# One pool of eight PSUM banks, and the transposes of a head pair in one run, in a two-layer hybrid attention block

## The chip, the cores and the metric

The kernel runs on one core of a Trainium2 chip. The metric is the device time of one execution in microseconds (us), the median of three runs. Engines are named as in the profile: PE (TensorE matmuls), PEld (TensorE weight loads), DVE (VectorE), ACT (ScalarE), POOL (GpSimd), SP (SyncE, whose queue issues the DMAs).

## The reference

The block has two layers over 256 tokens `x` and 256 context tokens `ctx`, 1024 features, float32. Each layer normalises and modulates its input, projects it, and computes three branches: neighbourhood attention with a bias (NA, 8 heads of 64), a gated MLP with spatial mixing, and latent attention (MLA, 8 heads of 96). The branches are merged by sigmoid gates, and a squared-ReLU MLP follows. The last layer updates only `x`. What the change touches is the softmax attention of both kinds:

```python
def dense_attention(q, k, v):
    ...
        s = jnp.einsum('bhqd,bhkd->bhqk', q_blk, k).astype(jnp.float32) * scale
        p = jax.nn.softmax(s, axis=-1).astype(v.dtype)
        return jnp.einsum('bhqk,bhkd->bhqd', p, v)
```

In layer 0 the 256 `x` queries see 512 keys (context and `x`) and the 256 context queries see the 256 context keys; in layer 1 there are only the `x` queries.

## The kernel before

**Tiles and stages.** Tokens are handled in tiles of 128. Every projection is three float32r matmuls per 128 rows of contraction (`mm3`, L286 to L289: high by high, high by low, low by high), with the weights split into a rounded part on ACT (L115) and a rest on DVE (L116). A layer runs: key, query and value projections (`gemm_b`, L305), the MLA latents, the gated MLP (`u` L716, `sg` L724), NA attention (L740 to L753), part of the merge (L757), the MLA keys and queries (L760 to L837), MLA attention (L842 to L849), the rest of the merge (L852 to L856), the output projection with the next norm (L887 to L914), and the MLP (L943 to L972).

**Attention.** `soft_pv` (L427) handles one pair of heads. For each stream `v` (stream 0: `x` queries with 4 key tiles; stream 1, in layer 0 alone: context queries with 2) and each query tile `qt` it writes the scores of both heads to PSUM (tile `S`, L438: two float32r matmuls per head in NA, L410 and L411; one float32 matmul per head, shown as two records, in MLA, L417). Then for each head: bias add on DVE (L443, NA and stream 0 alone), negated row maximum on DVE (L445), exponential with its sum on ACT (L448), reciprocal and scaling on DVE (L450, L451), transposes of the 2 or 4 key tiles on PE into a bank `pt` (L454), and a copy to the tile `PT` on ACT (L456). I call the two heads of one `qt` of one stream a unit. After both units of a stream the values are applied (L460, `pv` or `pvm`, 16 records for four key tiles and 8 for two), behind the copy of the last head (the dependency at L464). `P` and `PT` have two buffers each.

**Banks.** PSUM has eight banks of 128x512. `psum(tag, name)` (L47) takes one from a pool with four tags:

```python
return pp.tile([128, 512], F32, tag=tag, name=name, bufs={"mm": 4, "s": 2, "pt": 1, "pv": 1}[tag])
```

Tag `mm` serves all projections (`b_ps`, `u`, `gate`, `z`, `kv`, `qm`, `o_ps`, `f`) and the modulation sums; `s` serves the scores, the norm's sums `st_ps`, and all small transposes (`mod_t`, `tr_ps`, `c_tr`, `h_tr`) and `sg`; `pt` the transposed probabilities; `pv` the attention output and the broadcast norm `rstd_b`.

**What sets the order of the work.** A scheduler in the tile framework, run when the program is built, orders the instructions of each engine: of those that are ready, the one that the program traced first. Each engine then works its list in that order. Tiles of one tag get their banks in the order in which the program first writes them: the first write of a tile is not put ahead of the first write of an earlier tile of the same tag, even if banks are free. Tiles of other tags may pass. Matmuls that add to a tile which has been written already are not bound by this.

**What stands beside attention.** `merge` (L474) computes for each of eight output tiles a gate (24 matmuls, L488) and a `z` (12 matmuls, L492), all in tag `mm`. The merges are traced after the four head pairs, and each of their steps is queued behind the scores of a certain unit (`paced`, L301, with `tc.issue_after` in `gemm_a`, L298; the first 10 or 36 steps are free), so that they spread over the attention.

**The norm.** `norm_apply` (L279) and `norm_stream` (L232) reduce the sums of squares with a matmul (`st_ps`, L237), form the factor (DVE L239, POOL L241, DVE L244), and broadcast it with a matmul (`rstd_b`, L247). In the output projection (L887 to L914) and at the end of layer 0's MLP (L965 to L972) the norm of stream 0 is traced between the chunks of stream 0 and those of stream 1, and that of stream 1 after them. `mod_pooled` (L177) forms layer 1's modulation beside layer 0's MLP; its two ends put matmuls, two copies (L214) and transposes (L217) into PSUM tiles.

Of the kernel before, what the change touches and what calls it, by code (L numbers as in the profile page):

```python
# [7 lines left out]
F32 = mybir.dt.float32  # L8
F32R = mybir.dt.float32r
AF = mybir.ActivationFunctionType  # L10
ALU = mybir.AluOpType
# [15 lines left out]
def hybrid_block_kernel(tc, a, out):  # L27
    nc = tc.nc
    act = nc.scalar.activation
    vec = nc.vector  # L30
    mm = nc.tensor.matmul

    from contextlib import ExitStack, nullcontext
    with ExitStack() as es:
        def pool(name, bufs=1, **kw):
            return es.enter_context(tc.tile_pool(name=name, bufs=bufs, **kw))
# [8 lines left out]
        pp = pool("ps", space=PSUM)  # L45

        def psum(tag, name):  # L47
            return pp.tile([128, 512], F32, tag=tag, name=name, bufs={"mm": 4, "s": 2, "pt": 1, "pv": 1}[tag])


        def g2(name, dt=F32R):
# [21 lines left out]
        ident = cp.tile([128, 128], F32, name="ident")  # L73
# [66 lines left out]
        def mod_finish(ps, w, dsts, modT, bmod, streams):  # L140

            t = tmp2("mod_sb")
            vec.tensor_copy(t[:, :w], ps[:, :w])
            pst = psum("s", "mod_t")
            for i in range(w // 128):
                nc.tensor.transpose(pst[:, i * 128:(i + 1) * 128], t[:, i * 128:(i + 1) * 128], ident)
            for i in range(w // 128):
                v4 = pst[:, i * 128:(i + 1) * 128].rearrange("p (j r) -> p j r", j=4)
                for v in range(streams):
                    o, b = dsts(modT[:, v, :], i), dsts(bmod, i)  # L150
                    i0 = v4[:, :, v]
                    if len(o.shape) == 3:
                        i0 = i0.rearrange("p (a b) -> p a b", a=2)
                    vec.tensor_tensor(out=o, in0=i0, in1=b, op=ALU.add)

        def mod_quarter(l, q, modT, bmod, streams):

            ps = psum("pt", "mod_ps")
            for kb in range(4):
                for kk in range(2):  # L160
                    raw = g2("rawm", F32)
                    nc.sync.dma_start(out=raw, in_=a["wmod1"][l, q, kb][:, kk * 512:kk * 512 + 512])
                    mod_cols(ps, raw, 0, 128, 2 * kb + kk)
                yield
            mod_finish(ps, 128, lambda m, i: m[:, 0:16].rearrange("p (a c) -> p a c", a=2)[:, :, 2 * q:2 * q + 2], modT,
                       bmod, streams)

        def mod_group(l, g, modT, bmod, streams):
            ps = psum("mm", "mod_ps")
            for k in range(KC):  # L170
                raw = load(a["wmod"][l, g - 2, k])
                mod_cols(ps, raw, 0, 256, k)
                yield
            mod_finish(ps, 256, lambda m, i: m[:, 8 * g:8 * g + 8].rearrange("p (j i) -> p j i", i=2)[:, :, i], modT, bmod,
                       streams)
# [251 lines left out]
        def soft_pv(score, V, pv, streams, bias, marks):  # L427

            for v in range(streams):
                kts = [0, 1, 2, 3] if v == 0 else [2, 3]  # L430
                k0, nk = kts[0] * 128, 128 * len(kts)
                PT = [gp.tile([128, 4, NX], F32, tag="PT", name="PT", bufs=2) for _ in range(2)]
                for qt in range(2):
                    q0 = v * NX + qt * 128
                    S = []
                    for hh in range(2):
                        s = psum("s", "S")
                        marks.append(score[hh](s[:, :nk], q0, k0, nk).ins)  # L438
                        S.append(s)
                    for hh in range(2):  # L440
                        s = S[hh]
                        if bias is not None and v == 0:
                            vec.tensor_tensor(out=s[:, :NX], in0=s[:, :NX], in1=bias[hh][:, qt, :], op=ALU.add)  # L443
                        nm = sp.tile([128, 1], F32, tag="nm", name="nm")
                        vec.tensor_reduce(out=nm, in_=s[:, :nk], axis=AX.X, op=ALU.max, negate=True)  # L445
                        P = gp.tile([128, 512], F32, tag="P", name="P", bufs=2)
                        sm = sp.tile([128, 1], F32, tag="sm", name="sm")
                        act(out=P[:, :nk], in_=s[:, :nk], func=AF.Exp, bias=nm, accum_out=sm)  # L448
                        r = sp.tile([128, 1], F32, tag="r", name="r")
                        vec.reciprocal(r, sm)  # L450
                        vec.tensor_scalar(out=P[:, :nk], in0=P[:, :nk], scalar1=r, scalar2=None, op0=ALU.mult)  # L451
                        pt = psum("pt", "pt")
                        for i in range(len(kts)):
                            nc.tensor.transpose(pt[:, i * 128:(i + 1) * 128], P[:, i * 128:(i + 1) * 128], ident)  # L454
                        n = len(kts)
                        turned = act(out=PT[hh][:, :n, qt * 128:(qt + 1) * 128],  # L456
                                     in_=pt[:, :nk].rearrange("p (i q) -> p i q", i=n), func=AF.Copy)
                for i, kt in enumerate(kts):
                    for hh in range(2):
                        m = mm(pv[64 * hh:64 * hh + 64, v * NX:(v + 1) * NX], lhsT=V[kt][hh], rhs=PT[hh][:, i, :],  # L460
                               start=(i == 0), stop=(i == len(kts) - 1), tile_position=(0, 64 * hh))
                        if i == 0 and hh == 0:

                            tc.add_manual_dep(m.ins, turned.ins.name, mybir.DependencyInfo(  # L464
                                mybir.DependencyClass.Sync, mybir.DependencyReason.DATA), reason="both heads")
# [81 lines left out]
        for l in range(L):  # L547
# [114 lines left out]
            for t in range(4):  # L662
                vec.tensor_scalar(out=cnat[t][:, 0:128], in0=cnat[t][:, 0:128], scalar1=rsc[:, t:t + 1], scalar2=None,
                                  op0=ALU.mult)
                if t in tts:
                    vec.tensor_scalar(out=cnat[t][:, 160:416], in0=cnat[t][:, 160:416], scalar1=rsc[:, 4 + t:5 + t],
                                      scalar2=None, op0=ALU.mult)
# [72 lines left out]
            for j in range(4):  # L740
                bias = []
                for hh in range(2):
                    bt = gp.tile([128, 2, NX], F32, tag="bias", name="bias", bufs=2)
                    with tc.issue_after(last_load[0]):
                        nc.sync.dma_start(out=bt, in_=a["nab"][l, 2 * j + hh])
                    bias.append(bt)
                pv = psum("pv", "pv")
                soft_pv([na_score(kT, qT, 2 * j + hh) for hh in range(2)],
                        [[vna[t][:, (2 * j + hh) * 64:(2 * j + hh + 1) * 64] for hh in range(2)] for t in range(4)],
                        pv, ns, bias, marks)  # L750
                H, Lo = split_out(pv, "yna", T)
                ynH.append(H)
                ynL.append(Lo)  # L753
# [88 lines left out]
            for j in range(4):  # L842
                pv = psum("pv", "pvm")
                soft_pv([mla_score(kmT, qmT, 2 * j + hh) for hh in range(2)],
                        [[vml[t][:, (2 * j + hh) * 64:(2 * j + hh + 1) * 64] for hh in range(2)] for t in range(4)],
                        pv, ns, None, marks)
                H, Lo = split_out(pv, "yml", T)
                ymH.append(H)
                ymL.append(Lo)  # L849
# [36 lines left out]
            both = BOTH if ns == 2 else 0  # L886
# [11 lines left out]
            for n in range(both, 8):  # L898
                out_chunk(a["wa"][l, 28 + n], n, mixH, mixL, [0], 16, acc)
                if last:  # L900
# [3 lines left out]
                                             op0=ALU.mult, op1=ALU.subtract)  # L904
# [165 lines left out]
```

## Time and profile before

| | us |
|---|---|
| median of 3 runs (lowest to highest) | 1402.77 (1400.9 to 1403.62) |
| the profiled execution's own time | 1402.83 |
| its span in the trace | 1400.8 |
| PE busy | 1370.2 (98%) |
| DVE busy | 957.4 (68%) |
| ACT busy | 704.7 (50%) |

The span is the time from the first to the last instruction; 2.0 us of the profiled execution lie around it. PE's busy time counts a matmul to its modelled end, and a matmul overlaps the next one's start, so the start-to-start distances of a timeline are the finer measure. A line of the timeline reads: start, duration, engine, line of the kernel, operation, written and read tiles, shape, count, and in brackets idle time with what ended it.

### The profile page before, as it was taken

What the parts mean: (1) busy time and instruction counts of PE and PEld (TensorE: products, weight loads), DVE (VectorE), ACT (ScalarE), POOL (GpSimd) and SP (SyncE); (2) the same over time, 40 slices, a digit from 0 to 9 for tenths busy, and PEclk for the clock granted to TensorE, in tenths of its full rate; (3) what the DMA queues carried; (4) which work ended last, traced back from release to release, by engine and by line L of the source; (5) the groups of instructions that cost most, each with busy time, mean ns of one, the idle gap of its engine ahead of it and who ended that gap; (6) DMA issues with size and microseconds to landing.
All of it is one profiled execution on the core that took longest, in us unless ns stands there. A gap on an engine that the chain in (4) does not pass through costs nothing.

```text
span 1400.8 us, 22572 instructions
## 1 busy us (share of the span) xinstructions
PE 1370.2 (98%) x8438; PEld 1161.8 (83%) x8438; DVE 957.4 (68%) x2071; ACT 704.7 (50%) x1440; POOL 56.9 (4%) x35
## 2 busy tenths in 40 slices
PE   6999999999999999999999999999999999999999
PEld 4788767777676789988888888988888878999998
DVE  4666477665563558899766665786787766877775
ACT  3466256443453346623324233566676665656654
POOL 0110000110000000000000000011002100000000
PEclk9999999999999999999999999999999999999999
DMA  9423542234313465665555552443543434566664
GB/s 331 142 84 106 187 150 90 71 105 123 119 46 114 127 195 168 208 202 172 203 205 188 175 197 89 150 137 94 181 136 99 136 91 136 181 181 180 183 183 148
DMA packets 67214, 210.61 MB, mean 150 GB/s; under 512 B 8609, under 2 KB 9633, under 8 KB 67105
## 3 DMA queue, kind: packets, MB, share of 16 engines
q1 hardware_dynamic: 67104, 209.18, 46.6%
q8 instruction: 66, 1.08, 0.3%
q14 instruction: 44, 0.35, 0.1%
HBM read 208.10 MB, written 1.05 MB: 149 GB/s over the span
## 4 chain that ended last, share of the span: by engine, by line
PE 96%; DVE 1%; DMA 1%; ACT 1%; issue 0%; SPq 0%; POOL 0%; ACTq 0%; DVEq 0%
PE o_ps L287 8%; PE o_ps L289 8%; PE o_ps L288 8%; PE f L288 6%; PE f L287 6%; PE f L289 6%; PE gate L287 5%; PE gate L288 5%; PE gate L289 5%; PE b_ps L287 5%; PE b_ps L288 4%; PE b_ps L289 4%; PE pt L454 3%; PE S L417 2%; PE z L287 2%; PE z L289 2%
## 5 line engine op out<-in xcount | busy, mean ns | idle before, releaser
L115 ACT ACTIVATE wh<-raw 128x512 fp32r<-128x512 f32 (+1 forms) x570 | 353.1, 626 | 515.8 <-PE o_ps L288 179.7
L116 DVE TENSOR_TENSOR wl<-raw,wh 128x512 fp32r<-128x512 f32 (+1 forms) x570 | 385.8, 683 | 178.1 <-ACT wh L115 172.7
L289 PE MATMUL f<-hH,wl 128*128 128x258 f32 (+2 forms) x560 | 180.9, 324 | 0.1
L287 PE MATMUL f<-hH,wh 128*128 128x258 f32 (+2 forms) x560 | 180.4, 323 | 0.5 <-ACT wh L115 0.5
L288 PE MATMUL f<-hL,wh 128*128 128x258 f32 (+2 forms) x560 | 180.4, 324 | 0.2 <-DVE hL L277 0.2
L288 PE MATMUL o_ps<-aL,wh 128*128 128x256 f32 (+1 forms) x544 | 176.1, 327 | 0.0
L287 PE MATMUL o_ps<-aH,wh 128*128 128x256 f32 (+1 forms) x544 | 176.0, 328 | 0.0
L289 PE MATMUL o_ps<-aH,wl 128*128 128x256 f32 (+1 forms) x544 | 175.6, 328 | 0.0
L287 PE MATMUL gate<-hH,wh 128*128 128x512 f32 (+1 forms) x384 | 140.5, 366 | 0.0
L289 PE MATMUL gate<-hH,wl 128*128 128x512 f32 (+1 forms) x384 | 130.3, 339 | 0.0
L288 PE MATMUL gate<-hL,wh 128*128 128x512 f32 (+1 forms) x384 | 130.1, 339 | 0.0
L287 PEld LDWEIGHTS f<-hH,wh 128*128 128x128 f32 x560 | 106.0, 190 | 9.1 <-ACT wh L115 0.7
L289 PEld LDWEIGHTS f<-hH,wl 128*128 128x128 f32 x560 | 106.2, 190 | 8.5 <-DVE wl L116 0.3
L288 PEld LDWEIGHTS f<-hL,wh 128*128 128x128 f32 x560 | 105.9, 190 | 8.5 <-DVE hL L277 0.4
L287 PEld LDWEIGHTS o_ps<-aH,wh 128*128 128x128 f32 x544 | 102.7, 190 | 9.5 <-ACT aH L937 0.8
L288 PEld LDWEIGHTS o_ps<-aL,wh 128*128 128x128 f32 x544 | 103.1, 190 | 8.5
L289 PEld LDWEIGHTS o_ps<-aH,wl 128*128 128x128 f32 x544 | 102.7, 190 | 8.8
L288 PE MATMUL b_ps<-wl,hH 128*128 128x512 f32 (+2 forms) x288 | 108.8, 381 | 0.0
L289 PE MATMUL b_ps<-wh,hL 128*128 128x512 f32 (+2 forms) x288 | 106.3, 381 | 0.0
L287 PE MATMUL b_ps<-wh,hH 128*128 128x512 f32 (+2 forms) x288 | 103.7, 385 | 0.0
L200 DVE SCALAR_TENSOR_TENSOR macc<-rawx,sS,macc 128x512 f32<-128x512 f32 x112 | 78.9, 748 | 32.7 <-DMA rawx<-in_wmod_dram 32.4
L287 PEld LDWEIGHTS gate<-hH,wh 128*128 128x128 f32 x384 | 72.7, 189 | 15.9 <-issue 7.5
(229 smaller groups left out, 2481.3 us busy)
## 6 DMA issues: line engine op xcount, KB each, us to landing
raw<-in_wa_dram SPq DMA_DIRECT2D x147, 512.0 KB, 3.6
raw<-in_w_dram SPq DMA_DIRECT2D x68, 512.0 KB, 3.6
raw<-in_wb_dram SPq DMA_DIRECT2D x32, 512.0 KB, 3.3
raw<-in_wmod_dram SPq DMA_DIRECT2D x32, 512.0 KB, 3.4
rawx<-in_wmod_dram SPq DMA_DIRECT2D x32, 512.0 KB, 4.5
raw<-in_wo_dram SPq DMA_DIRECT2D x24, 512.0 KB, 3.6
rawm<-in_wmod_dram SPq DMA_DIRECT2D x32, 256.0 KB, 6.0
rawx<-in_wmod_dram SPq DMA_DIRECT2D x32, 256.0 KB, 4.2
```

The costliest lines, as they stand in the source:

```text
L115: act(out=wh[:, :width], in_=src, func=AF.Copy)
L116: vec.tensor_tensor(out=wl[:, :width], in0=src, in1=wh[:, :width], op=ALU.subtract)
L200: summed = vec.scalar_tensor_tensor(out=o, in0=src, scalar=s, in1=o, op0=ALU.mult, op1=ALU.add)
L287: mm(ps, lhsT=sh, rhs=mh, start=first, stop=False)
L288: mm(ps, lhsT=sh, rhs=ml, start=False, stop=False)
L289: mm(ps, lhsT=sl, rhs=mh, start=False, stop=last)
L417: return mm(s, lhsT=Q[h][0:96, q0:q0 + 128], rhs=K[h][0:96, k0:k0 + nk], start=True, stop=True)
L454: nc.tensor.transpose(pt[:, i * 128:(i + 1) * 128], P[:, i * 128:(i + 1) * 128], ident)
```

## The change

All PSUM tiles come from one tag with eight banks. In `soft_pv` the loop over the two heads is cut in two: the first does bias, maximum, exponential and scaling of both heads; the second does the transposes and copies of both. The first transpose of the unit gets a dependency on the scaling of the second head.

```diff
-            return pp.tile([128, 512], F32, tag=tag, name=name, bufs={"mm": 4, "s": 2, "pt": 1, "pv": 1}[tag])
+            return pp.tile([128, 512], F32, tag="bank", name=name, bufs=8)
...
+                    Ps = []
                     for hh in range(2):
                         s = S[hh]
...
-                        vec.tensor_scalar(out=P[:, :nk], in0=P[:, :nk], scalar1=r, scalar2=None, op0=ALU.mult)
+                        scaled = vec.tensor_scalar(out=P[:, :nk], in0=P[:, :nk], scalar1=r, scalar2=None, op0=ALU.mult)
+                        Ps.append(P)
+                    for hh in range(2):
+                        P = Ps[hh]
                         pt = psum("pt", "pt")
                         for i in range(len(kts)):
-                            nc.tensor.transpose(pt[:, i * 128:(i + 1) * 128], P[:, i * 128:(i + 1) * 128], ident)
+                            m = nc.tensor.transpose(pt[:, i * 128:(i + 1) * 128], P[:, i * 128:(i + 1) * 128], ident)
+                            if i == hh == 0:
+
+                                tc.add_manual_dep(m.ins, scaled.ins.name, mybir.DependencyInfo(
+                                    mybir.DependencyClass.Sync, mybir.DependencyReason.DATA), reason="both heads")
```

## Rows read from the trace of the kernel before

**Rows 1.** The page: busy time by engine, and the clock in 40 slices.

```profile
PE 1370.2 (98%) x8438; PEld 1161.8 (83%) x8438; DVE 957.4 (68%) x2071; ACT 704.7 (50%) x1440; POOL 56.9 (4%) x35
...
PEclk9999999999999999999999999999999999999999
```

**Rows 2.** Windows, four attention stretches; columns: width, busy PE, PEld, DVE, ACT, POOL, PEclk.

```profile
185.00:262.00 77.00, 73.95 (x438) 52.40 (x437) 58.09 (x155) 50.39 (x130) 3.63 (x2) 1.00 0.29 96
340.00:446.00 106.00, 106.00 (x573) 74.53 (x572) 55.52 (x136) 49.48 (x122) 0.00 (x0) 1.00 0.29 93
1015.00:1068.00 53.00, 49.11 (x350) 41.11 (x351) 39.75 (x98) 36.86 (x85) 1.85 (x2) 1.00 0.37 108
1105.00:1165.00 60.00, 56.34 (x379) 42.87 (x378) 34.84 (x77) 35.84 (x82) 0.00 (x0) 1.00 0.26 79
```

**Rows 3.** Layer 0: the last query parts on DVE, then PE's timeline before attention.

```profile
L401 DVE SCALAR_TENSOR_TENSOR naQL<-tr_ps,gq,naQ x16: 743/750/757, 100.3 to 119.1; 64x512 fp32r<-64x512 f32 x16
...
173.24 1.05 PE L724 MATMUL sg<-wsT,gv 128*128 128x128 f32 x8
...
174.79 0.51 PE L287 MATMUL gate<-hH,wh 128*128 128x512 f32 x1
...
181.54 0.39 PE L410 MATMUL S<-naK,naQ 128*128 128x512 f32 x1
```

**Rows 4.** One tile's instructions (`pt`): transposes and copies; ns min/median/max.

```profile
L454 PE MATMUL pt<-ident,P x320: 269/273/333, 189.7 to 1159.9; 128*128 128x128 f32 x160
L456 ACT ACTIVATE PT<-pt x96: 364/597/602, 190.3 to 1160.2; 128x512 f32<-128x512 f32 x64, 128x256 f32<-128x256 f32 x32
```

**Rows 5.** Timeline: one NA head with four key tiles, layer 1's last pair.

```profile
1055.30 0.48 PE L410 MATMUL S<-naK,naQ 128*128 128x512 f32 x1
...
1056.05 0.43 DVE L443 TENSOR_TENSOR S<-S,bias 128x256 f32<-128x256 f32 x1 [0.20 <-PE S L411]
...
1056.52 0.69 DVE L445 TENSOR_REDUCE nm<-S 128x1 f32<-128x512 f32 x1
...
1059.26 0.68 ACT L448 ACTIVATE P<-S,nm 128x512 f32<-128x512 f32 x1
...
1060.97 0.63 PE L454 MATMUL pt<-ident,P 128*128 128x128 f32 x4 [0.89 <-DVE P L451]
...
1062.28 1.95 PE L460 MATMUL pv<-PT,vna 128*64 128x256 f32 x16 [0.69 <-ACT PT L456]
```

**Rows 6.** Timeline: one MLA head's scores and their maximum, layer 1.

```profile
1154.38 1.02 PE L417 MATMUL S<-kml,qml 96*128 96x512 f32 x2
...
1155.44 0.69 DVE L445 TENSOR_REDUCE nm<-S 128x1 f32<-128x512 f32 x1 [0.60 <-PE S L417]
```

**Rows 7.** Timeline: NA heads with two key tiles, layer 0.

```profile
216.28 0.28 PE L411 MATMUL S<-naK,naQL 128*128 128x256 f32 x1
...
216.60 0.42 DVE L445 TENSOR_REDUCE nm<-S 128x1 f32<-128x256 f32 x1 [1.13 <-PE S L411]
...
216.70 0.47 ACT L448 ACTIVATE P<-S,nm 128x256 f32<-128x256 f32 x1
...
217.49 0.35 DVE L451 TENSOR_SCALAR P<-P,r 128x256 f32<-128x256 f32 x1
```

**Rows 8.** Timeline: the norm of stream 0 in layer 0's output projection.

```profile
534.87 0.48 DVE L869 SCALAR_TENSOR_TENSOR xT<-o_ps,modT,xT 128x256 f32<-128x256 f32 x1 [0.16 <-PE o_ps L289]
...
536.08 0.42 DVE L256 TENSOR_TENSOR acc<-acc,sq 128x256 f32<-128x256 f32 x1
...
538.07 0.46 DVE L244 TENSOR_SCALAR diag<-ident,rs 128x128 f32<-128x128 f32 x2
```

**Rows 9.** Timeline: the first projection's matmuls, before and after the clock rose.

```profile
24.82 0.63 PE L287 MATMUL b_ps<-wh,hH 128*128 128x512 f32 x1
...
26.96 0.39 PE L287 MATMUL b_ps<-wh,hH 128*128 128x512 f32 x1
27.19 0.40 PE L288 MATMUL b_ps<-wl,hH 128*128 128x512 f32 x1
```

## The prediction, made before the change was run

> **What bounds the kernel now.** I read the page first: PE is busy 98% of the span, DVE 68%, ACT 50% [rows 1]. So the question is where PE can gain or lose time, and that is asked stage by stage. The windows over the four attention stretches come next [rows 2]: PE is busy 73.95 of 77, 106.00 of 106, 49.11 of 53 and 56.34 of 60 us. The reader is to see how little idle there is: 3.05 + 0 + 3.89 + 3.66 = 10.6 us. That is all a freer supply of banks could win there. Attention by itself would not fill PE: a unit waits for a chain of DVE and ACT steps. The gates and `z` of the merge fill these waits.
>
> Why they can is the third view [rows 3]. The queries of layer 0's NA are finished at about 119.9 us, but the first scores (tag `s`) start at 181.54, behind the last `sg` tiles (also `s`) at 173.24. The gate (tag `mm`), which the program traces after all scores of this attention, starts at 174.79 and passes them. The four tags are four independent orders; within one, first writes keep the program's order.
>
> **The change, part by part.** *One tag.* Eight banks for anyone also means one order for all first writes. The program's order in attention is: scores of both heads of a unit, their transposes, scores of the next unit, transposes, values; and after four pairs the first gate. So the next unit's scores may not be written before this unit's transposes, and no gate before the last transposes. I forecast that PE then stands still through every unit's softmax, and that the gates run afterwards, at their old cost, with nothing beside them. The work on PE is the same; the idle time is added. Its price is the chain from the rows, for the kinds of unit. The copies count 64 heads with four key tiles and 32 with two [rows 4], so 32 long and 16 short units, half of each NA and half MLA.
>
> Long NA unit, from its first score matmul: bias of head 0 after 0.75 us (1055.30 to 1056.05), maximum 0.47 later, lasting 0.69 [rows 5]; so 1.22 to 1.91. DVE then does bias 1 at 1.93 and maximum 1 at 2.40 to 3.09. The exponential of head 1 starts at 3.11, and from its start to the first transpose the bare case shows 1059.26 to 1060.97, 1.71 us [rows 5]. The transposes start at 4.82. PE had work for four 512-column matmuls at 0.23 (26.96 to 27.19 in [rows 9]) and about 0.1 for the first weights, 1.02. Idle: 3.8 us.
>
> Long MLA unit: one head's scores hold PE for 0.86 (1.02 as shown, less the 0.16 by which a matmul's modelled end overlaps the next: 0.39 shown and 0.23 apart in [rows 9]), and the maximum starts 1.06 after them [rows 6]. For head 1: 0.86 + 1.06 = 1.92, plus 0.71 to the exponential, plus 1.71 makes 4.34; less 1.72 of scores, 2.6 idle.
>
> Short units: maximum 0.32 after the second score matmul, lasting 0.42; from the exponential to the end of scaling 216.70 to 217.84, 1.14 [rows 7], and a handover of about 0.14. With the two exponentials following each other on ACT (0.47 and the read of the sum), the NA unit starts its transposes at 2.65 after 0.5 of scores (2.15 idle), the MLA unit at 2.85 after 0.86 (2.0 idle).
>
> *The values.* They follow the copies of both heads. From the start of a head's transposes to the values 1060.97 to 1062.28, 1.31 [rows 5]; a second copy of 0.60 in a row on ACT [rows 4] makes 1.91. Four transposes are shown as 0.63 and one as 0.27 [rows 4, 5], so they start 0.11 apart and eight take 0.88: PE waits 1.03. That holds for the 16 stream-0 groups, whose values are a first write that the next scores wait for. The 8 stream-1 groups write a tile that is in use already, so their 1.06 us of values (half of 1.95, with the switch) slip into the next unit's wait.
>
> *The transposes in one run.* Moving head 0's four transposes and copy behind head 1's scaling costs 4 x 0.11 = 0.44 us a long unit where nothing else runs; it is in the sums above. What the pair of banks saves, the wait of the second transposes for the first copy, is part of the 10.6 us.
>
> Sum for attention: 16 x 3.8 + 16 x 2.6 + 8 x 2.15 + 8 x 2.0 + 16 x 1.03 - 8 x 1.06 = 143.6. The idle time there now goes: -10.6.
>
> *The norms.* Chunks of stream 1 fill the wait for stream 0's norm today. In one order they may not be first written before `st_ps` and `rstd_b`. From the last chunk's end about 0.25 to the update at 534.87, 1.63 to the end of L256 at 536.50, 2.03 to the end of the diagonal at 538.53 [rows 8]: 3.9 us, three times (twice in layer 0, once in layer 1). Behind stream 1's norm in layer 0 only `st_ps` is a first write: 1.9 + 0.1, twice. Together 15.7. The two ends of `mod_pooled` put two copies of a bank on DVE (0.7 each, by the maximum of 512 columns in [rows 5]) and their transposes in front of the next chunk: some 1.5 us each, 3.0. The bounds for this part are 0 (the scheduler finds other ready matmuls of open tiles) and 30 (DVE is late by its own queue).
>
> *Without a term:* the small transposes gain banks (`h_tr` and `tr_ps` have two today), and the start of layer 0 loses some, as the modulation sums must wait for the first norm; a few us either way, in the range. No DMA is moved on SP except that weight loads for the gates stop at three raw buffers while attention runs; the gates that follow take 5.5 us per 512 KB in layer 0, slower than the loads. DVE and ACT have room: a long NA unit needs 3.5 us of DVE in 5.7.
>
> 143.6 - 10.6 + 15.7 + 3.0 = 151.7. On the profiled execution's 1402.83, which is 0.06 over the median: **1555 us**.
>
> **The rivals.** *The clock falls (0.15).* The granted clock is 9 tenths or more in every slice [rows 1], and PE is busy in all of them. Only at the start, after little work, a matmul of 512 columns shows 0.63 us, and after a run of matmuls 0.39 [rows 9]: the two levels, 1.2 and 2.4 GHz. In the changed attention PE would work under half of the time. If the low level came, PE's own attention work would about double. That work is 320 transposes of 0.11, 24 value groups (16 x 1.95 + 8 x 1.06), NA scores of 18.6 and MLA scores of 34.4, 127 us; the NA part, with the longest waits, is 55. So 1610 to 1680. The Trainium skill, in "TensorE: Matmul & The Clock Gate" (section "What's actually happening"), says that the throttled state is the default and that activity releases it; by that rule the time would be these 1610 to 1680 us, against 1555 at the full clock. The trace of before has no stretch of this kind to agree or disagree; its waits of up to 1 us in a row of bare steps at 1059 to 1062 us left the clock alone [rows 2, 5], so I keep the full clock for the sum.
>
> *Only the gates are held back (0.06).* If scores of the next unit pass this unit's transposes, softmax overlaps softmax, and the bound is the larger of DVE and PE per unit: DVE 3.54 against PE 2.77 in a long NA unit, PE in MLA. Then idle is some 16 us, plus about 5 us of start in each of four attentions; with the norms 1447 us. Against it: [rows 3] show no later tile of a tag in front of an earlier one.
>
> *Not slower: the order stays as it is (0.05).* If banks went to whichever tile is ready, gates would still pass the scores. Its place is the wait between a unit's scores and its transposes, and it decides as soon as one gate matmul stands there. Then the change wins at most the 10.6 us and some late scores: 1390 us. A change without effect, where the order comes out as today, gets 0.02.
>
> **How the numbers follow.** The forecast has 0.72. A unit's idle may be off by half a microsecond, and there are 48: 24 us to each side. With the bounds of the norms that makes 1505 to 1595 for the forecast alone; to leave no more than 2 in 10 out it is stretched into the milder half of the clock's case: 1500 to 1630. Faster by over 0.2% (about what a measurement of this kernel can tell from no change) 0.05, same 0.02, slower 0.93.
>
> **What would show it.** Right: in the timeline no `gate` or `z` between a unit's `S` and its `pt`; PE idle of 3 to 4 us before the transposes of NA units, released by the scaling (L451), about 2.6 in MLA; PE busy near 40% in NA stretches; gates in a block behind the last pair; o_ps idle before `st_ps`. Wrong: gates between scores and transposes as now, PE still near 98%, or the clock below 9 in attention. An idle time per unit below 2 us would mean that scores do run ahead.

## The result: slower by 17%, and the profile after

The changed kernel takes 1647.07 us (median of 4 runs, 1646.44 to 1648.05) where the kernel before takes 1403.19 (4 runs): a ratio of 1.1737, 95% interval 1.1714 to 1.1761. So it is slower, as forecast, but by 244 us and not by 152, and above the range of 1500 to 1630.

The page of the changed kernel: busy time by engine, and the granted clock in 40 slices. They answer to [rows 1]. In the views of the changed kernel the exponential is at L449, the scaling at L452, the transposes at L458, the copies at L464 and the values at L468.

```profile
PE 1468.3 (89%) x8438; PEld 1220.0 (74%) x8438; DVE 972.8 (59%) x2071; ACT 717.4 (44%) x1440; POOL 56.9 (3%) x35
...
PEclk9999867997679999999999999999669769999999
```

PE runs the same 8438 instructions, yet is busy 98 us longer, in a span that is 243.6 us longer. The clock row suggests why: in the slices of attention the granted clock has fallen to 6 to 8 tenths.

Windows over the four attention stretches of the changed kernel, from the first scores to the first gates (columns as in [rows 2]):

```profile
178.70:281.70 103.00, 59.26 (x262) 38.21 (x260) 48.34 (x134) 39.68 (x103) 0.00 (x0) 0.70 0.05 16
376.30:480.60 104.30, 70.61 (x260) 38.96 (x258) 38.75 (x107) 38.38 (x101) 0.00 (x0) 0.71 0.00 1
1151.00:1223.70 72.70, 41.38 (x164) 27.06 (x162) 31.75 (x82) 25.90 (x56) 0.00 (x0) 0.62 0.08 23
1289.20:1365.00 75.80, 52.88 (x162) 27.89 (x160) 22.02 (x51) 24.93 (x56) 0.00 (x0) 0.64 0.00 1
sum 355.80, PE 224.14 PEld 132.13 DVE 140.87 ACT 128.89 POOL 0.00; mean PE 56.03 PEld 33.03 DVE 35.22 ACT 32.22 POOL 0.00
```

No gate stands in these stretches; SP's transfers, which bring the gates' weights, all but stop (16, 1, 23 and 1 GB/s, against 79 to 108 in [rows 2]). PE idles 355.8 - 224.1 = 131.7 us. The forecast idle time was 143.6. But the stretches as a whole, forecast as 143.6 + 127 = 271 us, take 356. (The 127 counts matmuls from start to start and the 224 of PE to their modelled ends, so these two are not to be compared with each other.)

Two views show how. First PE's timeline in layer 1, two long NA units in a row (columns: start us, us, engine line op out<-in xcount, in brackets the idle time before and its releaser):

```profile
1205.90 0.50 PE L410 MATMUL S<-naK,naQ 128*128 128x512 f32 x1
...
1206.70 0.40 PE L411 MATMUL S<-naK,naQL 128*128 128x512 f32 x1
1210.72 1.94 PE L458 MATMUL pt<-ident,P 128*128 128x128 f32 x8 [3.63 <-DVE P L452]
1212.32 0.77 PE L410 MATMUL S<-naK,naQ 128*128 128x512 f32 x1
...
1213.74 0.63 PE L411 MATMUL S<-naK,naQL 128*128 128x512 f32 x1
1217.46 1.94 PE L458 MATMUL pt<-ident,P 128*128 128x128 f32 x8 [3.09 <-DVE P L452]
```

From the first score to the transposes the first of these units takes 4.82 us, what the prediction had built out of [rows 5]. Its scores are shown as 0.40, the upper level of [rows 9]. Then PE waits 3.63 us. The eight transposes behind the wait take 1.94, where [rows 5] has 0.63 for four, and the next unit's scores are shown as 0.63, the lower level. The clock fell during the wait.

Second, layer 0: values and the first gates behind the last pair.

```profile
269.42 3.68 PE L468 MATMUL pv<-PT,vna 128*64 128x256 f32 x16 [0.69 <-ACT PT L464]
...
279.22 1.09 PE L458 MATMUL pt<-ident,P 128*128 128x128 f32 x4 [1.98 <-DVE P L452]
...
281.68 0.80 PE L287 MATMUL gate<-hH,wh 128*128 128x512 f32 x1
...
282.70 0.63 PE L289 MATMUL gate<-hH,wl 128*128 128x512 f32 x1
...
283.93 0.40 PE L289 MATMUL gate<-hH,wl 128*128 128x512 f32 x1
284.16 0.39 PE L287 MATMUL gate<-hH,wh 128*128 128x512 f32 x1
```

Sixteen value matmuls take 3.68 us against 1.95 in [rows 5]. The first gate comes only after the last transposes, and further on in that block the gates run at 0.39 again.

Where the 243.6 us of span lie can be read off the first score matmul of NA and the first matmul of `o_ps` in each layer. Between them are the attention and its gates; all else is the rest.

| us | before | after | longer by |
|---|---|---|---|
| layer 0, first scores to first `o_ps` | 181.5 to 500.8: 319.3 | 178.7 to 625.5: 446.8 | 127.5 |
| layer 1, the same | 1010.3 to 1188.4: 178.1 | 1151.0 to 1426.0: 275.0 | 96.9 |
| the rest of the span | 903.4 | 922.6 | 19.2 |

The forecast was 143.6 - 10.6 = 133.0 for attention and 15.7 + 3.0 = 18.7 for the rest. The rest is right, and the whole miss of 91 us lies in the 224.4 of attention.

### The profile page after: what moved, and what is told of

Read it like the earlier page. It is cut to its first block, busy times and chain, and to the rows that moved or that the text cites. A ratio compares the mean times of both kernels' runs of the same rounds, so it can differ in the third digit from the quotient of the medians.

```text
span 1644.4 us, 22574 instructions
## 1 busy us (share of the span) xinstructions
PE 1468.3 (89%) x8438; PEld 1220.0 (74%) x8438; DVE 972.8 (59%) x2071; ACT 717.4 (44%) x1440; POOL 56.9 (3%) x35
## 4 chain that ended last, share of the span: by engine, by line
PE 77%; issue 12%; DVE 7%; ACT 3%; DMA 1%; SPq 0%; POOL 0%; POOLq 0%; ACTq 0%; DVEq 0%
PE o_ps L288 6%; PE o_ps L287 6%; PE o_ps L289 6%; PE f L287 5%; PE f L288 5%; PE f L289 5%; PE b_ps L287 4%; PE b_ps L288 4%; PE b_ps L289 4%; PE gate L287 4%; PE pt L458 3%; PE gate L289 3%; PE gate L288 3%; DVE nm L446 2%; PE pv L468 2%
## 5 line engine op out<-in xcount | busy, mean ns | idle before, releaser
L458 PE MATMUL pt<-ident,P 128*128 128x128 f32 x320 | 70.6, 388 | 120.6 <-DVE P L452 115.1
L458 PEld LDWEIGHTS pt<-ident,P 128*128 128x128 f32 x320 | 54.8, 201 | 149.3 <-issue 111.7
L287 PE MATMUL gate<-hH,wh 128*128 128x512 f32 (+1 forms) x384 | 133.4, 347 | 0.0
L446 DVE TENSOR_REDUCE nm<-S 128x1 f32<-128x512 f32 (+1 forms) x96 | 56.9, 600 | 112.5 <-PE S L417 79.2
L289 PEld LDWEIGHTS f<-hH,wl 128*128 128x128 f32 x560 | 106.9, 191 | 8.2
```

The costliest lines, as they stand in the source:

```text
L287: mm(ps, lhsT=sh, rhs=mh, start=first, stop=False)
L289: mm(ps, lhsT=sl, rhs=mh, start=False, stop=last)
L458: m = nc.tensor.transpose(pt[:, i * 128:(i + 1) * 128], P[:, i * 128:(i + 1) * 128], ident)
```

## The experiments

The theory: the one order holds gates and scores back (the forecast), and in the waits the clock falls, which makes PE's own attention work dearer. The rivals: waiting for both heads, that is the transposes of a pair in one go, is what costs; or the units' chains are longer than forecast and the clock plays no part. Each experiment's ratio is to the kernel before, run beside it on the same chip.

### The two parts of the change, one at a time

The second part alone, on the four old tags:

```diff
-            return pp.tile([128, 512], F32, tag="bank", name=name, bufs=8)
+            return pp.tile([128, 512], F32, tag=tag, name=name, bufs={"mm": 4, "s": 2, "pt": 1, "pv": 1}[tag])
```

> The kernel before, with its four tags, and of the change only the second part: the transposes of a pair of heads in one go behind the second head's scaling. If the one order of the single tag makes the loss (theory), the gates still stand between a unit's scores and its transposes here, the granted clock stays at 1.0 in attention, and the time is 1403 to 1440 us: the second transposes wait for the first copy in the only bank, and the pair's chain is longer, but PE has gates to fill it. If waiting for both heads makes the loss (rival), the time is above 1500 us, and PE's idle time before the transposes is 3 to 4 us a unit.

Measured: 1451.36 us, ratio 1.0353 (1.0327 to 1.0378), between the two expectations. The clock is not what is lost here: it is granted at 0.994 over the run.

The first part alone, one tag, with each head's transposes behind its own scaling (against the changed kernel):

```diff
-                    Ps = []
...
-                    for hh in range(2):
-                        P = Ps[hh]
...
-                            m = nc.tensor.transpose(pt[:, i * 128:(i + 1) * 128], P[:, i * 128:(i + 1) * 128], ident)
-                            if i == hh == 0:
...
+                            nc.tensor.transpose(pt[:, i * 128:(i + 1) * 128], P[:, i * 128:(i + 1) * 128], ident)
```

> The changed kernel without its second part: one tag of eight banks, and each head's transposes behind its own scaling, as before. Theory (the one order holds the gates back, and the fallen clock makes PE's own attention work dearer): 1610 to 1640 us, since head 0's four transposes lie beside head 1's softmax again, 0.44 us in each of 32 long units and 0.22 in each of 16 short ones at the full clock, 17.6 us together and up to twice that at the low level; granted clock in attention 0.6 to 0.8 as in the changed kernel. Rival (waiting for both heads makes the loss): back at 1403 to 1440 us.

Measured: 1607.91 us, ratio 1.1475 (1.1439 to 1.1511), 2 us under the theory's span. From the first scores to the last transposes the granted clock is 0.66 and 0.69 in the two NA, 0.87 and 0.69 in the two MLA. The one tag makes most of the loss: 206 us by itself. The one go costs 49 us on the old tags and 39 on top of the one tag, more than I had given it in either place.

### Is it the clock?

The changed kernel with useless work: seven banks in the tag, and in the eighth a tile `heat` into which matmuls are written that nothing reads.

```diff
-            return pp.tile([128, 512], F32, tag="bank", name=name, bufs=8)
+            return pp.tile([128, 512], F32, tag="bank", name=name, bufs=7)
...
+        heat = pp.tile([128, 512], F32, tag="heat", name="heat", bufs=1)
...
+                    warm = {(True, 0): 12, (False, 0): 9, (True, 1): 7, (False, 1): 6}[bias is not None, v]
+                    with tc.issue_after(marks[-1]):
+                        for _ in range(warm):
+                            mm(heat, lhsT=hH[0][:, 0:128], rhs=hH[0][:, 0:512], start=True, stop=True)
```

> The changed kernel with seven banks in its tag, and in the eighth bank 12, 9, 7 or 6 matmuls of 512 columns (long NA, long MLA, short NA, short MLA units), whose result nothing reads, behind each unit's second scores: they fill the wait for the softmax with work that is of no use. Theory (of the changed kernel's 131.7 idle and 92 further us, most of the 92 are the clock's): the granted clock in attention is 0.95 to 1.0, and the time falls although PE does more, to 1555 to 1590 us. Rival (the clock has no part, the units' chains are simply longer than forecast): no change or slower, 1645 to 1690 us, with the chain from the first scores to the transposes of a long NA unit well above 4.82 us.

Measured: 1576.59 us, ratio 1.1245 (1.1223 to 1.1266). With 440 more matmuls the kernel is 70 us faster than the changed one. Its four attention stretches:

```profile
179.20:266.90 87.70, 74.22 (x414) 54.78 (x412) 48.36 (x134) 38.52 (x103) 0.00 (x0) 0.96 0.06 19
360.60:442.90 82.30, 74.22 (x380) 49.31 (x378) 39.29 (x107) 37.01 (x101) 0.00 (x0) 1.00 0.00 1
1115.10:1174.50 59.40, 48.66 (x259) 36.39 (x258) 31.93 (x82) 25.35 (x58) 0.00 (x0) 0.94 0.10 31
1240.10:1294.70 54.60, 49.17 (x233) 30.58 (x232) 22.60 (x51) 23.78 (x56) 0.00 (x0) 0.96 0.00 1
sum 284.00, PE 246.26 PEld 171.06 DVE 142.18 ACT 124.66 POOL 0.00; mean PE 61.57 PEld 42.77 DVE 35.55 ACT 31.17 POOL 0.00
```

The stretches are 355.8 - 284.0 = 71.8 us shorter, the whole gain, at a granted clock of 0.94 to 1.00 in place of 0.62 to 0.71. DVE and ACT do the same work. Nor is the chain of a unit longer than forecast, but for the first of each NA (see below). A long NA unit of layer 1 in this kernel (L412 and L413 scores, L464 transposes):

```profile
1160.81 0.50 PE L412 MATMUL S<-naK,naQ 128*128 128x512 f32 x1
...
1161.85 2.90 PE L445 MATMUL heat<-hH 128*128 128x512 f32 x12
1165.39 1.09 PE L464 MATMUL pt<-ident,P 128*128 128x128 f32 x8 [0.63 <-DVE P L458]
```

From the first score to the transposes it takes 4.58 us, against 4.82 forecast, and the useless matmuls end before the scaling does. So 70 of the 91 us are the clock's.

The same, with the useless matmuls in the units of NA alone:

```diff
-                    warm = {(True, 0): 12, (False, 0): 9, (True, 1): 7, (False, 1): 6}[bias is not None, v]
+                    warm = {(True, 0): 12, (False, 0): 0, (True, 1): 7, (False, 1): 0}[bias is not None, v]
```

> The kernel with the useless matmuls, but in the units of NA alone; the units of MLA wait without them. Between no such matmuls (1647 us) and all of them (1577 us) lie 70 us. If the clock falls in both attentions (theory), MLA's share by PE's own work, 72 of 127 us, stays lost: 1612 to 1622 us, with a granted clock of 0.6 to 0.75 in the MLA stretches and over 0.95 in NA. If the longer waits of NA alone make it fall (rival): 1577 to 1590 us.

Measured: 1614.39 us, ratio 1.1498 (1.1466 to 1.1530). Its four windows, NA and MLA in turn:

```profile
178.20:265.80 87.60, 73.69 (x413) 54.41 (x411) 48.34 (x134) 38.47 (x103) 0.00 (x0) 0.98 0.06 19
359.60:460.50 100.90, 68.05 (x260) 36.07 (x258) 38.40 (x107) 38.03 (x101) 0.00 (x0) 0.73 0.00 0
1132.90:1192.60 59.70, 49.06 (x260) 36.74 (x258) 31.90 (x82) 25.17 (x58) 0.00 (x0) 0.94 0.10 32
1258.40:1333.20 74.80, 52.82 (x163) 27.32 (x161) 22.16 (x51) 24.69 (x56) 0.00 (x0) 0.64 0.00 1
```

Where PE has filler the clock stays, where it waits 2.6 us a unit by forecast it falls too: 0.73 and 0.64. Both attentions pay, MLA 1614.4 - 1576.6 = 38 us of the 70. This kernel has seven banks in its tag too, and its MLA windows are 100.9 and 74.8 us, against 104.3 and 75.8 with eight: the bank that went to `heat` is not where the gain comes from.

The useless matmuls with each head's transposes behind its own scaling (10, 7, 5, 4 of them, on the kernel of the first part alone, with seven banks and the tile `heat` as above):

```diff
...
+                    warm = {(True, 0): 10, (False, 0): 7, (True, 1): 5, (False, 1): 4}[bias is not None, v]
```

> One tag, useless matmuls in the waits (10, 7, 5 or 4 of them a unit), and each head's transposes behind its own scaling again, not in one go. Theory (at the full clock the one go costs 0.44 us in a long unit and 0.22 in a short one, 17.6 us in all, and the rest of the 39 us that it cost beside one tag was the clock): 1555 to 1563 us. Rival (the one go costs its 39 us at any clock): 1535 to 1542 us.

Measured: 1555.00 us, ratio 1.1083 (1.1055 to 1.1111). With the clock near the upper level in both (0.986 and 0.989 over the run) the one go costs 1576.6 - 1555.0 = 21.6 us, near the 17.6 forecast; as far as these two pairs show, the rest of its 39 us beside the one tag came with the clock.

### The norms

```diff
-            return pp.tile([128, 512], F32, tag="bank", name=name, bufs=8)
+            return pp.tile([128, 512], F32, tag=name if name in ("st_ps", "rstd_b") else "bank", name=name, bufs=1 if name in ("st_ps", "rstd_b") else 6)
```

> The changed kernel with the two small tiles of the norms in tags of their own (one bank each, six for the rest). Theory (the one order makes PE wait at each norm, 15.7 us by the prediction): 1625 to 1635 us, and the idle time before the column sums falls from 21 us to under 12, and before the spread of the norm from 6.9 to under 2. Rival (the norms' waits are made up later, or are the queue of DVE): 1642 us or more.

Measured: 1617.52 us, ratio 1.1527 (1.1510 to 1.1545). First the two groups of the changed kernel, by line (busy time, mean ns of one, idle time before and its releasers):

```profile
L247 PE MATMUL rstd_b<-diag,ones 128*128 128x256 f32 x14 | 6.6, 564 | 6.9 <-DVE diag L244 6.9
...
L237 PE MATMUL st_ps<-ones,acc 128*128 128x1 f32 x28 | 5.0, 283 | 21.0 <-DVE gq L604 12.2 <-DVE acc L256 8.8
```

And the same groups with the norms apart:

```profile
L247 PE MATMUL rstd_b<-diag,ones 128*128 128x256 f32 x14 | 5.4, 475 | 0.5 <-DVE diag L244 0.5
...
L237 PE MATMUL st_ps<-ones,acc 128*128 128x1 f32 x28 | 4.5, 266 | 0.0
```

The stops are gone. Of the 21.0 us, 12.2 are PE's first wait of the kernel, which only passes to another tile; the other 8.8 and the 6.9 make 15.7. By the stages of the table the rest of the span is 903.3 us, as before the change: the 19.2 are these stops. Another 10 us came off in attention (711.6 against 721.8), where this edit only takes two banks from the one tag; the mean granted clock of the run is 0.932 against 0.919. What let it fall less there stays open.

Near the upper level, useless matmuls and norms apart together (five banks left for the one tag):

```diff
-            return pp.tile([128, 512], F32, tag="bank", name=name, bufs=7)
+            return pp.tile([128, 512], F32, tag=name if name in ("st_ps", "rstd_b") else "bank", name=name, bufs=1 if name in ("st_ps", "rstd_b") else 5)
```

> The kernel with the useless matmuls (1577 us), and the norms' two small tiles in tags of their own, five banks left for the rest. At the lower clock the norms' own tags were worth 29 us. Theory (part of that was the clock; at the full clock PE's stops at the norms are the 15.7 us of the prediction): 1558 to 1564 us. Rival (the stops are worth 29 us at any clock): 1545 to 1550 us. Five banks too few: above 1577 us.

Measured: 1560.72 us, ratio 1.1124 (1.1092 to 1.1155): 15.9 us less, the 15.7 of the prediction.

### Which tiles must pass which

Gates and projections in a tag of their own, all else in the other four banks:

```diff
-            return pp.tile([128, 512], F32, tag="bank", name=name, bufs=8)
+            return pp.tile([128, 512], F32, tag="mm" if tag == "mm" else "bank", name=name, bufs=4)
```

> The changed kernel with the gates' and projections' tag apart (four banks), and scores, transposes, values and small sums in one tag of the other four; the transposes of a pair still in one go. Theory (what costs is that nothing fills the waits): gates stand between scores and transposes again, clock 1.0, time 1395 to 1425 us, though the next unit's scores still keep behind this unit's transposes. Rival (it is the scores that may not run ahead): the time stays above 1550 us.

Measured: 1461.88 us, ratio 1.0423 (1.0401 to 1.0446). Letting the gates pass takes back 185 of the 244 us, but 37 us more than I expected are left. PE's costliest wait in that kernel:

```profile
L458 PE MATMUL pt<-ident,P 128*128 128x128 f32 x320 | 44.8, 280 | 38.0 <-DVE P L452 36.6 <-ACT th L498 1.0 <-ACT wh L115 0.3
```

With the next unit's scores still behind this unit's transposes, only gates and `z` stand in between: in this kernel's timeline 3 to 12 matmuls in most units of layer 0, and 21 to 24 of half the width in most units of layer 1. In many units they do not last until the scaling is done.

This kernel has the transposes in one go, and the one go by itself had cost 49 us on the old tags. Beside that kernel (1451.36 us) it is only 10.5 us slower. So once the gates may pass, most of what is left belongs to the one go, which the expectation had not counted.

The scores alone in a tag of their own:

```diff
-            return pp.tile([128, 512], F32, tag="bank", name=name, bufs=8)
+            return pp.tile([128, 512], F32, tag="S" if name == "S" else "bank", name=name, bufs=2 if name == "S" else 6)
```

> The changed kernel with the scores alone taken out of the one tag (a tag of two banks of their own; the other six banks stay one tag), so the gates are still held back behind the last transposes, but the next unit's scores may run ahead of this unit's transposes. If the cost of the one order is that one unit's softmax cannot overlap the next one's (theory), 1447 us at the full clock, by the rival of the prediction, and up to 1500 us where the clock falls; PE idle in the long NA units about 1 us a unit. If it is that gates cannot fill the waits, whatever the scores do (rival), above 1570 us and the clock in attention still 0.6 to 0.8.

Measured: 1534.22 us, ratio 1.0935 (1.0908 to 1.0962). Between the two expectations: neither holds by itself. The waits that are left:

```profile
L458 PE MATMUL pt<-ident,P 128*128 128x128 f32 x320 | 50.3, 303 | 19.5 <-DVE P L452 19.1
...
L417 PE MATMUL S<-kml,qml 96*128 96x512 f32 (+1 forms) x96 | 47.8, 590 | 19.9 <-ACT P L449 19.8
...
L410 PE MATMUL S<-naK,naQ 128*128 128x512 f32 (+1 forms) x48 | 24.2, 504 | 23.5 <-ACT P L449 23.5
```

The scores wait for their two banks until an exponential has read them. What the tag of the scores gains has two sources, as the windows of layer 0 show, NA and then MLA, from the first scores to the last transposes:

```profile
106.90:256.70 149.80, 127.29 (x645) 93.49 (x644) 86.23 (x216) 73.75 (x178) 2.64 (x2) 0.89 0.24 85
354.60:421.00 66.40, 52.57 (x253) 28.36 (x251) 37.73 (x101) 33.01 (x96) 0.00 (x0) 0.95 0.00 1
```

In MLA the window has 253 matmuls, two more than in the changed kernel, so nothing new fills the waits; softmax overlaps softmax, and the window is 66.4 us long against 102.9, at a granted clock of 0.95 against 0.71. In NA the scores now also pass the projections and the gated MLP: they start at 106.9 us and not at 178.7, and some 390 matmuls of `b_ps`, `u`, `sg` and others fill the waits. So this run is no clean price of the overlap alone. Taken out one at a time, gates give back 185 us and scores 113.

### The old tags with two banks for transposes and values

The kernel before, with one change:

```diff
-            return pp.tile([128, 512], F32, tag=tag, name=name, bufs={"mm": 4, "s": 2, "pt": 1, "pv": 1}[tag])
+            return pp.tile([128, 512], F32, tag="pt" if tag == "pv" else tag, name=name, bufs={"mm": 4, "s": 2, "pt": 2, "pv": 2}[tag])
```

> The kernel before with one thing changed: the bank of the transposes and that of the values become one tag of two, heads in their old loop. If a freer supply of banks is worth something in attention: 1392 to 1401 us, since the transposes no longer wait for the copy of the head before (2.9 us in the trace of before) and the idle time there is 10.6 us in all. Rival (one order for both tiles takes back what the second bank gives): 1401 to 1410 us.

Measured: 1408.10 us, ratio 1.0041 (1.0026 to 1.0056): the rival, 0.4% slower. PE's idle time before transposes falls from 4.8 to 2.9 us, and before NA's scores it rises from 1.8 to 4.0. A second bank that these two tiles share is worth nothing in the kernel before. Whether a bank of its own for one of them would be, was not tried.

The same tags with the transposes of a pair in one go (the loops of the changed kernel):

> Transposes of a pair in one go on the old tags, with two banks shared by transposes and values. With one bank the one go cost 49 us, and PE stood 25.6 us before second transposes, waiting for the copy of the first. Theory (the only bank is what makes the one go dear on the old tags): 1400 to 1420 us, and that wait is under 5 us. Rival (holding head 0's transposes back costs by itself, through the later end of each pair): 1435 to 1455 us.

Measured: 1444.94 us, ratio 1.0301 (1.0287 to 1.0316): the rival again. First the group of transposes with one bank (the second part alone), then three groups with two:

```profile
L458 PE MATMUL pt<-ident,P 128*128 128x128 f32 x320 | 53.6, 282 | 29.9 <-ACT PT L464 25.6 <-DVE P L452 4.2
```

```profile
L458 PE MATMUL pt<-ident,P 128*128 128x128 f32 x320 | 47.8, 276 | 12.0 <-ACT PT L464 7.3 <-DVE P L452 4.4
...
L417 PE MATMUL S<-kml,qml 96*128 96x512 f32 (+1 forms) x96 | 44.8, 549 | 8.9 <-ACT P L449 8.7 <-ACT qml L804 0.2
...
L410 PE MATMUL S<-naK,naQ 128*128 128x512 f32 (+1 forms) x48 | 20.8, 433 | 12.6 <-ACT P L449 12.6
```

The second bank takes the wait for the copy from 25.6 to 7.3 us, and 21.3 us stand in front of the next scores, which wait for an exponential; with one bank these were 3.6. Two steps of the timeline of this kernel show what may stand ahead of it:

```profile
197.13 0.60 ACT L464 ACTIVATE PT<-pt 128x512 f32<-128x512 f32 x1 [1.64 <-PE pt L458]
197.63 0.47 ACT L449 ACTIVATE P<-S,nm 128x256 f32<-128x256 f32 x1
...
198.08 0.60 ACT L464 ACTIVATE PT<-pt 128x512 f32<-128x512 f32 x1
...
198.24 0.39 PE L410 MATMUL S<-naK,naQ 128*128 128x256 f32 x1 [0.71 <-ACT P L449]
```

The pair's copies now come together on ACT, the exponential behind the first of them, and the scores behind that exponential. That this order on ACT makes the whole 42 us is read from the trace and was not tried by itself.

## Why the prediction was right in sign and too small

- **The order.** Right. In the changed kernel no gate and no `z` stands between a unit's scores and its transposes, and none before the last pair. The kernel with gates apart, 185 us faster, shows that most of the loss hangs on this.
- **The idle time of a unit.** Right. The chain of the long NA unit shown above is 4.82 us, and PE idles 131.7 us in the four stretches against 143.6. The first NA unit of each layer is longer than the sum had it: PE idles 8.10 us in layer 0 and 5.49 in layer 1, since steps of the gated part (`yg`) stand among its softmax on ACT and DVE, and since ACT loads a table for 1.28 us just ahead of the first exponential. The kernel before has this load in the same place, but there gates and `z` kept PE busy beside it (8.49 of 9.50 us from 181.5 to 191.0). Against 3.8 each, 6 us were missing in the sum. The loads and the first transposes of NA in each layer, in the timeline of the changed kernel:

```profile
183.86 1.28 ACT L449 ACT_TABLE_LOAD   x1
...
187.96 1.97 PE L458 MATMUL pt<-ident,P 128*128 128x128 f32 x8 [8.10 <-DVE P L452]
...
1153.12 1.28 ACT L449 ACT_TABLE_LOAD   x1
...
1157.65 1.94 PE L458 MATMUL pt<-ident,P 128*128 128x128 f32 x8 [5.49 <-ACT yg L740]
```

- **The clock: the step that failed.** "I keep the full clock for the sum" put 0 where the runs show 70 us (1647.1 against 1576.6 with PE kept busy). I took waits of up to 1 us in a row as evidence for waits of 3 to 4 us; [rows 2] held nothing of that kind. The rival had the mechanism and a chance of 0.15. Its price, 55 to 127 us, holds the 70, though neither of its two ends happened: both attentions paid, NA 33 us and MLA 38, and the clock did not stay down, but changed between the levels, 0.62 to 0.71 on the mean. With that goes that PE was busy 58% and 57% of the NA stretches (59.26 of 103.00 and 41.38 of 72.70 us), and not near 40%. The rule of the Trainium skill ("TensorE: Matmul & The Clock Gate", "What's actually happening"), that the throttled state is the default and activity releases it, spoke against the sum. The trace of the changed kernel agrees with it: 0.63 us for a matmul of 512 columns after a wait, 0.40 after a run of gates. I should have given it the larger chance.
- **The rest of attention.** With the clock held, attention is 150.9 us longer than before (648.3 in the kernel with useless matmuls, 497.4 before), against 133.0 forecast. Some 13 of these 18 us lie in the four stretches (284.0 against 143.6 + 127): the two first units are 6 of them, and three of the windows still show a clock of 0.94 to 0.96. The other 12 are not split further.
- **The values and the one go.** The 17.6 us in the sum measured 21.6 near the upper level and 39 where the clock falls. That the one go would cost 42 to 49 us on the old tags, where gates do fill PE's waits, I had not forecast. With one bank PE waits 25.6 us for the copy of the first head's transposes; with two, 21.3 us in front of the next scores.
- **The norms and the modulation.** 18.7 forecast, 19.2 measured; 15.7 for the norms, 15.9 measured near the upper level. With the norms apart the rest of the span is as before, so little is left for the 3.0 of the modulation.
- **The milder rival.** "Only the gates are held back", 1447 us, did not happen. The kernel that was built for it, with two banks for the scores, takes 1534: its price had left out that scores need their banks back from the exponentials, and that the clock falls there too (0.89 and 0.95 in the windows above). More banks for the scores were not tried.

The sum with the two missing terms: 1402.8 + 133.0 + 18.7 + 70 + 18 = 1642.5, of 1647.1. The 70 and the 18 come from the one run with useless matmuls, so the sum shows where the time went and is no check of it.

## What to carry to other kernels

A pool with one tag is one order: before merging tags, list which tiles pass each other now, and what fills the busiest engine's waits because of it. Where a change puts waits of some microseconds into a stretch of TensorE, cost the work that stays there at both clock levels, and don't take shorter waits in the old trace as evidence that the clock will hold. To tell a lost clock from a longer chain, fill the waits with useless matmuls that end before the wait does: if the time falls and the granted clock rises, the clock was part of the loss.

## What the runs showed that was not expected

440 matmuls whose result nothing reads made the kernel 70 us faster, and took the granted clock in attention from 0.62 to 0.71 up to 0.94 to 1.00. After a wait of 3.63 us in a unit the next matmuls ran at the lower level. And a second bank, shared by transposes and values, gave nothing: 1.9 us less of one wait, 2.2 more of another, 5 us slower in all.
